# Delta rule by pairs of heads: two heads' chunk work side by side in shared tiles

## The chip, the cores and the metric

The kernel runs on one core of a Trainium2 chip. Times are device microseconds (us) of that core, from the start to the end of one execution. The core has a matrix engine (TensorE, PE in the profile, with its weight loads as PEld), a vector engine (VectorE, DVE), a scalar engine (ScalarE, ACT), GpSimd (POOL) and SyncE (SP), which here only issues DMAs. Each engine works through its own queue in order.

## The reference

One decoder layer over 1024 positions of width 1024, batch 1: half a SwiGLU step, a mixer, half a SwiGLU step, and a final RMSNorm. The change touches only the mixer's first half, eight heads of a gated delta rule with keys and values of width 128 (the other half, a state-space scan of 16 heads, and the SwiGLU steps stay as they are):

```python
qkv = jax.nn.silu(causal_dwconv(gdn_qkv, gdn_conv_w))
beta = jax.nn.sigmoid(gdn_b)
g = -jnp.exp(gdn_a_log) * jax.nn.softplus(gdn_a + gdn_dt_bias)
o = gated_delta_rule(q, k, v, g, beta)
o = rms_norm(o, gdn_norm_w) * jax.nn.silu(gdn_z)
...
# S_t = exp(g_t) (I - beta_t k_t k_t^T) S_{t-1} + beta_t k_t v_t^T,  o_t = S_t^T q_t
decay = jnp.exp(jnp.where(incl, gc[..., :, None] - gc[..., None, :], -jnp.inf))
a_low = jnp.where(strict, beta[..., :, None] * kk * decay, 0.0)
t_inv = triangular_solve(eye + a_low, eye)
...
def step(state, inp):
    v_new = u_c - w_c @ state
    o = qd_c @ state + qk_c @ v_new
    state = state * gt_c + kd_c.T @ v_new
```

Queries and keys are normalised first. The kernel works on chunks of 128 positions, eight per head, rather than the reference's 64; the recurrence over chunks is the same.

## The kernel before

The program is written as engine instructions on tiles. A planner puts the instructions of each engine in a fixed order: what comes earlier in the source goes first, and what is ready by its reckoning may fill the gaps. It also sets the semaphores, and a tile with fewer buffers than its uses makes a new use wait for the release of an old one.

The projections of the normalised input, which is kept in `hhi` and `hlo` (the value rounded, and the rest), are made by `proj_half`: a half is 128 output channels by 512 positions, eight steps of three matmuls (`mm3`, L121 to L123) into one bank `ps_pj`, of which there are three. Weights come by `next_w`, two tiles of 128 channels at a time, in the order of `w_seq`: for a head first Q and K, then V and the gate Z. `conv_silu` (L781 to L789) projects two halves, evicts each with two ScalarE operations (L781, L782), adds three taps on VectorE (L784, 128x1024 each) and applies SiLU.

For each head h in turn, the loop in the section `gdn` then does the following.

1. **Decays** (L1125 to L1130): the running log decay `g_scr[h]` is loaded into `dt`, spread over the partitions; `qe` is its exponential times `qt`; GpSimd masks `dt` (L895) and ScalarE takes the exponentials of its eight blocks (L1129).
2. **Keys' products** (L1141 to L1155): for two chunks at a time into one bank `ps_mx` (there are two) kk and kq; VectorE takes the trace (`jd`, L1145), forms `br` and makes `u`, the triangular matrix, and writes the masked kq products back into `dt`.
3. **Inverse**: the diagonal 32x32 blocks of `u` go through DRAM (`fs_u`, `fu`) into a layout in which a substitution of 31 steps, two VectorE operations each (L1205, L1207), solves all of them at once; the result returns through `fs_x` to `lv` and `u` (L1210, L1217, L1218). Then the blocks are joined, first to 64, then to 128, by four runs of small products (L1225/L1226, L1232 to L1234, L1246, L1251) with copies between them.
4. **Transposes**: of `qt` for its norm (L1173), of the values into `vr` (L1186, L1188), of the keys into `kd` (L1262, L1264).
5. **Scan** over the eight chunks (L1274 to L1296): the product of keys with the state `st`, the correction `rr`, the product with the inverse, `vn`, the output `po` (one bank `ps_oo`) and the new state `sn`; the output replaces the values in `vr`.
6. **Norm** (L1302 to L1307): sums of squares, a reciprocal root by Newton steps, and the store of `vr` to `mix_scr`.

All products of steps 2 to 5 are in full fp32, and each such product of 128 columns is two TensorE instructions. Tiles of pool `g2` (`qe`, `dt`, `u`, `vr` and the small ones) have two buffers, `kt` three, `qt` two (tag `xst`); `vt_`, `kd`, `fu`, `fx`, `lv` have one. So the scan of one head stands beside the projections and the inverse of the next.

After the last projections `out_start` begins the output projection: `group_tile` for the four groups of state-space heads, `pair_prep` and `pair_tile` for two halves of four delta rule heads. These read `mix_scr` and the gates `z_scr` through `out_load` (tiles `nat`, `zg` in a pool of their own, `natp`) and add to `xt2`, eight blocks of x from a pool `x2`.

Of the kernel before, what the change touches and what calls it, by code (L numbers as in the profile page):

```python
# [11 lines left out]
F32 = mybir.dt.float32  # L12
# [9 lines left out]
P = 128  # L22
# [18 lines left out]
NEG = -1.0e30  # L41


@with_exitstack
def kernel(
# [1007 lines left out]
    def out_load(grp):  # L1053
        nat = natp.tile([P, NB, 256], F32, name="nat")
        nc.sync.dma_start(out=nat, in_=mix_scr[grp])
        zg = natp.tile([P, 2, L], F32, name="zg")
        for j in range(2):
            nc.sync.dma_start(out=zg[:, j], in_=z_scr[2 * grp + j])
        return nat, zg
# [40 lines left out]
    natp = cn.enter_context(tc.tile_pool(name="natp", bufs=1, side="right", reuse_waits="tile"))  # L1100
    with ExitStack() as cg:
        g1 = cg.enter_context(tc.tile_pool(name="gdn1", bufs=1, reuse_waits="tile"))
        g2 = cg.enter_context(tc.tile_pool(name="gdn2", bufs=2, reuse_waits="tile"))
        for h in range(GH):
            hl = h % 2
            qt = gp.tile([P, L], F32, name="qt", tag="xst", bufs=2)
            kt = g2.tile([P, L], F32, name="kt", bufs=3)
            vt_ = g1.tile([P, L], F32, name="vt_")
            wa = next_w()
            conv_silu(g1, wa, 0, cw_g, h, qt)  # L1110
            conv_silu(g1, wa, 1, cw_g, 8 + h, kt)
            wa = next_w()
            conv_silu(g1, wa, 0, cw_g, 16 + h, vt_)
            zc = g1.tile([P, L], F32, name="zc")
            for half in range(2):
                A.activation(out=zc[:, half * 512:(half + 1) * 512], in_=proj_half(*wa, 1, half),
                             func=AF.Silu)
            nc.sync.dma_start(out=z_scr[h], in_=zc)
            if h == GH - 1:
                out_start()  # L1120


            qe = g2.tile([P, L], F32, name="qe")
            dt = g2.tile([P, NB, P], F32, name="dt")
            nc.sync.dma_start(out=dt, in_=g_scr[h].rearrange("(b t) -> b t", b=NB).partition_broadcast(P))  # L1125
            A.activation(out=qe, in_=dt.rearrange("p b t -> p (b t)"), func=AF.Exp)
            causal(dt, (NB,))
            for b in range(NB):
                A.activation(out=dt[:, b], in_=dt[:, b], func=AF.Exp, bias=ngc[:, b, h:h + 1])  # L1129
            V.tensor_tensor(out=qe, in0=qe, in1=qt, op=ALU.mult)  # L1130


            u = g2.tile([P, NB, P], F32, name="u")
            tk = g2.tile([P, NB], F32, name="tk")
            br2 = g2.tile([P, NB], F32, name="br2")
            for b0 in range(0, NB, 2):
                pg = psum("mx")
                b2 = slice(b0, b0 + 2)
                for i in range(2):
                    bs = slice((b0 + i) * P, (b0 + i + 1) * P)  # L1140
                    T.matmul(pg[:, i * 256:i * 256 + P], lhsT=kt[:, bs], rhs=kt[:, bs], start=True, stop=True)  # L1141
                    T.matmul(pg[:, i * 256 + P:(i + 1) * 256], lhsT=kt[:, bs], rhs=qt[:, bs],
                             start=True, stop=True)
                    jd = g1.tile([P, P], BF16, name="jd")
                    V.scalar_tensor_tensor(out=jd, in0=pg[:, i * 256:i * 256 + P], scalar=1.0, in1=ident,  # L1145
                                           op0=ALU.mult, op1=ALU.mult,
                                           accum_out=tk[:, b0 + i:b0 + i + 1])
                V.tensor_scalar(out=tk[:, b2], in0=tk[:, b2], scalar1=EPS, scalar2=None, op0=ALU.add)
                V.reciprocal(out=br2[:, b2], in_=tk[:, b2])
                V.tensor_tensor(out=br2[:, b2], in0=br2[:, b2], in1=beta[:, b2, h], op=ALU.mult)  # L1150
                for i in range(2):
                    V.scalar_tensor_tensor(out=u[:, b0 + i], in0=pg[:, i * 256:i * 256 + P],
                                           scalar=br2[:, b0 + i:b0 + i + 1], in1=dt[:, b0 + i],
                                           op0=ALU.mult, op1=ALU.mult)
                V.tensor_tensor(out=dt[:, b2],  # L1155
                                in0=pg.rearrange("p (i c) -> p i c", i=2)[:, :, P:2 * P],
                                in1=dt[:, b2], op=ALU.mult)
            fs_u = dram.tile([4, NB, 32, 32], F32, name="fs_u", bufs=2)
            for j in range(4):
                js = slice(32 * j, 32 * j + 32)  # L1160
                nc.sync.dma_start(out=fs_u[j].rearrange("b s l -> s b l"), in_=u[js, :, js])


            vr = g2.tile([P, NB, P], F32, name="vr")
            ssq = g2.tile([P, NB], F32, name="ssq")
            rin = g2.tile([P, NB], F32, name="rin")
            rsqrt_into(g2, rin, tk, "rst")
            V.tensor_tensor(out=rin, in0=rin, in1=tk, op=ALU.mult)
            for half in range(2):
                pt = psum("mx")  # L1170
                for i in range(4):
                    b = half * 4 + i
                    T.transpose(pt[:, i * P:(i + 1) * P], qt[:, b * P:(b + 1) * P], ident)  # L1173
                for i in range(4):
                    b = half * 4 + i
                    jk = g2.tile([P, P], BF16, name="jk", bufs=1)
                    A.activation(out=jk, in_=pt[:, i * P:(i + 1) * P], func=AF.Square,
                                 accum_out=ssq[:, b:b + 1])
            cq = g2.tile([P, NB], F32, name="cq")
            V.tensor_scalar(out=cq, in0=ssq, scalar1=EPS * P, scalar2=EPS * EPS * P,  # L1180
                            op0=ALU.mult, op1=ALU.add)
            for half in range(2):
                pt = psum("mx")
                for i in range(4):
                    b = half * 4 + i
                    T.transpose(pt[:, i * P:(i + 1) * P], vt_[:, b * P:(b + 1) * P], ident)  # L1186
                hb = slice(half * 4, half * 4 + 4)
                V.tensor_tensor(out=vr[:, hb], in0=pt.rearrange("p (i c) -> p i c", i=4),  # L1188
                                in1=rin[:, hb].unsqueeze(2).to_broadcast([P, 4, P]), op=ALU.mult)


            fs_x = dram.tile([4, NB, 32, 32], F32, name="fs_x", bufs=2)
            fu = g1.tile([P, 32, 32], F32, name="fu")
            for q in range(4):
                nc.sync.dma_start(out=fu[32 * q:32 * q + 32], in_=fs_u.rearrange("j b s l -> (j b) s l"))
            fx = g1.tile([P, 8, 32], F32, name="fx")
            ft = g1.tile([P, 80], F32, name="ft")
            fxf = fx.rearrange("p s l -> p (s l)")
            G.memset(fxf, 0.0)
# [286 lines left out]
```

## Time and profile before

| | us |
|---|---|
| median of 3 runs | 2312.65 |
| lowest, highest | 2310.45, 2313.74 |
| the profiled execution | 2311.71 |
| its span, first to last instruction | 2309.8 |
| VectorE in the substitution, lines 1205 and 1207, 248 operations each | 51.9 and 53.5 |
| scan: VectorE's `rr`, `vn`, `sn` (lines 1276, 1281, 1293) | 19.6, 22.3, 16.6 |
| projections of the mixer, lines 121 to 123 with `hhi` and `hlo`, 2496 matmuls | 332.8, 332.2, 334.3 |

A row of groups gives line, engine, operation, what is written and read, count, busy time, mean of one in ns, and the idle time of the engine ahead of it. A row of the timeline gives start, length, engine, line, operation and count; matmuls are pipelined, so their lengths overlap and the distance of their starts tells what one costs. In a stretch of the view by windows the columns are length, busy time and count of each engine, granted clock, DMA share and rate.

### The profile page before, as it was taken

The numbers are of one execution on the slowest core, as the hardware profiler recorded it, in microseconds if no ns is written. First come the engines' busy times: TensorE is split into PE (matmuls) and PEld (weight loads), VectorE is DVE, ScalarE is ACT, GpSimd is POOL, SyncE is SP. The second block draws the span as 40 slices with busy tenths as digits, with TensorE's granted clock in tenths as the row PEclk, the third lists the DMA queues.
The fourth block names the chain that finished last, engine by engine and source line by source line (L and its number), as shares of the span: only waits on it lengthen the run. The fifth ranks groups of instructions, "written<-read, shape, count | busy, mean of one in ns | idle before, by whom it ended". The sixth has DMA issues, their size and how long they took to land.

```text
span 2309.8 us, 31485 instructions
## 1 busy us (share of the span) xinstructions
PE 2275.9 (99%) x11766; PEld 1868.7 (81%) x11766; DVE 1726.7 (75%) x3349; ACT 1096.0 (47%) x1990; POOL 53.6 (2%) x125
## 2 busy tenths in 40 slices
PE   7999999999999999999999999999999999999998
PEld 5788888888878888888888888888878888888886
DVE  7977776767765675668778888778698777766787
ACT  7433333343367785864455556422543333334344
POOL 0000000000000100000000000000000000000000
PEclk9999999999999999999999999999999999999999
DMA  3333332573652322222333222335223333329456
GB/s 111 125 114 103 105 108 98 175 279 129 220 180 78 92 92 74 72 86 74 83 101 82 73 83 61 116 98 192 91 83 116 111 102 105 109 88 349 141 156 214
DMA packets 220957, 281.33 MB, mean 122 GB/s; under 512 B 47008, under 2 KB 153564, under 8 KB 219780
## 3 DMA queue, kind: packets, MB, share of 16 engines
q1 hardware_dynamic: 220548, 279.23, 37.4%
q8 instruction: 92, 1.51, 0.3%
q14 instruction: 61, 0.50, 0.1%
q0 software_dynamic: 256, 0.10, 0.0%
HBM read 211.55 MB, written 67.73 MB: 121 GB/s over the span
## 4 chain that ended last, share of the span: by engine, by line
PE 89%; DVE 5%; ACT 2%; DMA 1%; issue 1%; SPq 0%; POOL 0%; DVEq 0%; ACTq 0%
PE ps_pj L123 11%; PE ps_pj L122 10%; PE ps_pj L121 10%; PE ps_pj L332 6%; PE ps_pj L334 6%; PE ps_pj L333 6%; PE ps_mx L332 3%; PE ps_mx L334 3%; PE ps_mx L333 3%; PE ps_pj L553 2%; PE ps_pj L554 2%; PE ps_pj L552 2%; PE ps_oo L334 2%; PE ps_oo L333 2%; PE ps_oo L332 2%; PE ps_sc L552 1%
## 5 line engine op out<-in xcount | busy, mean ns | idle before, releaser
L123 PE MATMUL ps_pj<-hhi,wlo 128*128 128x512 f32 x832 | 334.3, 402 | 0.0
L121 PE MATMUL ps_pj<-hhi,whi 128*128 128x512 f32 x832 | 332.8, 400 | 0.4 <-ACT gsb L826 0.4
L122 PE MATMUL ps_pj<-hlo,whi 128*128 128x512 f32 x832 | 332.2, 399 | 0.0
L334 PE MATMUL ps_pj<-bh,al 128*128 128x512 f32 x688 | 267.9, 389 | 0.0
L333 PE MATMUL ps_pj<-bl,ah 128*128 128x512 f32 x688 | 267.8, 389 | 0.0
L332 PE MATMUL ps_pj<-bh,ah 128*128 128x512 f32 x688 | 267.5, 390 | 0.0
L121 PEld LDWEIGHTS ps_pj<-hhi,whi 128*128 128x128 f32 x832 | 156.7, 188 | 28.8 <-ACT gsb L826 0.8
L123 PEld LDWEIGHTS ps_pj<-hhi,wlo 128*128 128x128 f32 x832 | 156.7, 188 | 28.5 <-issue 0.7
L122 PEld LDWEIGHTS ps_pj<-hlo,whi 128*128 128x128 f32 x832 | 156.7, 188 | 27.9
L239 ACT CAST ah<-wst 128x512 fp32r<-128x512 f32 x88 | 54.6, 622 | 210.8 <-PE ps_oo L333 125.3
L239 ACT CAST hid<-hraw 128x1024 fp32r<-128x1024 f32 (+1 forms) x84 | 82.3, 981 | 145.5 <-PE ps_oo L554 60.6
L333 PEld LDWEIGHTS ps_pj<-bl,ah 128*128 128x128 f32 x688 | 129.2, 188 | 26.8
L334 PEld LDWEIGHTS ps_pj<-bh,al 128*128 128x128 f32 x688 | 129.1, 188 | 26.6
L332 PEld LDWEIGHTS ps_pj<-bh,ah 128*128 128x128 f32 x688 | 128.9, 188 | 26.6
L315 DVE TENSOR_TENSOR as<-wst 128x512 f32<-128x512 f32 x220 | 145.0, 684 | 2.1 <-DMA wst<-in_ffn_w_up_dram 1.8
L240 DVE TENSOR_TENSOR al<-as,ah 128x512 fp32r<-128x512 f32 x220 | 141.0, 685 | 5.0 <-ACT ah L239 4.5
L332 PE MATMUL ps_mx<-bh,ah 128*128 128x512 f32 x352 | 138.6, 396 | 3.8 <-ACT m L341 1.4
L333 PE MATMUL ps_mx<-bl,ah 128*128 128x512 f32 x352 | 138.2, 393 | 0.4 <-DVE bl L240 0.4
L334 PE MATMUL ps_mx<-bh,al 128*128 128x512 f32 x352 | 137.7, 391 | 0.3 <-DVE al L240 0.3
L239 ACT CAST ah<-as 128x512 fp32r<-128x512 f32 x220 | 125.0, 617 | 20.8 <-DVE as L315 20.8
L240 DVE TENSOR_TENSOR hid<-hraw,hid 128x1024 fp32r<-128x1024 f32 (+1 forms) x84 | 95.0, 1131 | 32.8 <-ACT hid L239 32.5
L341 ACT COPY m<-ps_pj 128x512 f32<-128x512 f32 x88 | 51.5, 588 | 123.1 <-PE ps_pj L334 120.9
(448 smaller groups left out, 5118.9 us busy)
## 6 DMA issues: line engine op xcount, KB each, us to landing
hraw<-hid_scr SPq DMA_DIRECT2D x70, 512.0 KB, 4.4
hid_scr<-hs SPq DMA_DIRECT2D x110, 256.0 KB, 2.3
wst<-in_ffn_w_down_dram SPq DMA_DIRECT2D x50, 512.0 KB, 4.7
wst<-in_ffn_w_gate_dram SPq DMA_DIRECT2D x22, 1024.0 KB, 5.7
wst<-in_ffn_w_up_dram SPq DMA_DIRECT2D x22, 1024.0 KB, 5.4
wst<-in_w_in_dram SPq DMA_DIRECT2D x36, 512.0 KB, 5.2
hid_scr<-sg SPq DMA_DIRECT2D x44, 256.0 KB, 2.0
keep<-in_ffn_w_down_dram SPq DMA_DIRECT2D x20, 512.0 KB, 6.2
```

Source lines behind the costliest of these rows:

```text
L121: T.matmul(o, lhsT=wh, rhs=mh, start=first, stop=False)
L122: T.matmul(o, lhsT=wh, rhs=ml, start=False, stop=False)
L123: T.matmul(o, lhsT=wl, rhs=mh, start=False, stop=last)
L239: return (A.copy(out=hi, in_=src), V.tensor_tensor(out=lo, in0=src, in1=hi.bitcast(F32), op=ALU.subtract))
L240: V.tensor_tensor(out=lo, in0=src, in1=hi.bitcast(F32), op=ALU.subtract))
L315: V.tensor_tensor(out=t, in0=v[0], in1=v[1], op=v[2])
L332: T.matmul(bank, lhsT=wh[:, k], rhs=bh[:, k], start=a, stop=False, skip_group_check=True)
L333: T.matmul(bank, lhsT=wh[:, k], rhs=bl[:, k], start=False, stop=False, skip_group_check=True)
L334: T.matmul(bank, lhsT=wl[:, k], rhs=bh[:, k], start=False, stop=z, skip_group_check=True)
L341: A.copy(out=t, in_=bank)
L552: T.matmul(bank, lhsT=hh, rhs=wh, start=first and k == 0, stop=False, skip_group_check=True)
L553: T.matmul(bank, lhsT=hh, rhs=wl, start=False, stop=False, skip_group_check=True)
```

## The change

The loop over eight heads becomes a loop over four pairs. All tiles of a head's steps 1 to 6 get a dimension for the two heads, and the order of a pair is: Q and K of the first head, Q and K of the second, V of both from one weight tile, and then gates. The gates are taken from earlier pairs by `Z_BEHIND`: none in the first pair, those of heads 0 and 1 in the second, 2 and 3 in the third, 4 to 7 in the last.

- Keys' products: both banks `ps_mx` are filled, one for each head, sixteen instructions in a row; the small operations on `tk` and `br2` work on both heads.
- Substitution: the same 62 operations on twice the columns. The DMAs through DRAM stay of the same size each, twice as many for a pair.
- Levels of the inverse: runs of 16 chunks in place of 8; the two last levels fill two banks `ps_sc`.
- Scan: the products of both heads stand next to each other in one bank, and `vn` is one operation; `rr` and `sn` are two. `behind` adds a wait: the first product of a run waits for the results of both heads.
- Buffers: `qe`, `dt`, `u`, `vr`, `vt_` lie in a new pool `g3` with one buffer each, for two heads; `kt` alternates between `g3` and `g1`.
- `natp` and `x2` are gone. `nat` and `zg` take over the tiles of `vt` and `kt` in `g3`, the x blocks those of `qe`, `dt`, `u` and `vr`, loaded by `load_x2` at the same place of the program.

The core of the diff:

```diff
+Z_BEHIND = ((), (0,), (2,), (4, 6))
...
-    for h in range(GH):
-        w_seq.append((COL_Q + h * P, COL_K + h * P))
-        w_seq.append((COL_V + h * P, COL_GZ + h * P))
+    for h in range(0, GH, 2):
+        w_seq.extend((COL_Q + i * P, COL_K + i * P) for i in (h, h + 1))
+        w_seq.append((COL_V + h * P, None))
+        w_seq.extend((COL_GZ + i * P, None) for i in Z_BEHIND[h // 2])
...
-        nat = natp.tile([P, NB, 256], F32, name="nat")
+        nat = g3.tile([P, NB, 256], F32, name="nat", tag="vt")
...
-    natp = cn.enter_context(tc.tile_pool(name="natp", bufs=1, side="right", reuse_waits="tile"))
+    g3 = cn.enter_context(tc.tile_pool(name="gdn3", bufs=1, side="right", reuse_waits="tile"))
...
-        for h in range(GH):
+        for pr in range(GH // 2):
+            h0 = 2 * pr
+            kt2 = (g1, g3)[pr % 2 == 0].tile([P, 2, L], F32, name="kt", tag="kt")
+            kts = [kt2[:, i] for i in range(2)]
+            for i, h in enumerate((h0, h0 + 1)):
+                wa = next_w()
+                qts.append(gp.tile([P, L], F32, name="qt", tag="xst", bufs=2))
+                conv_silu(g1, wa, 0, cw_g, h, qts[-1])
+                conv_silu(g1, wa, 1, cw_g, 8 + h, kts[i])
             wa = next_w()
+            vt2 = g3.tile([P, 2, L], F32, name="vt_", tag="vt")
+            for i in range(2):
+                conv_silu(g1, wa, i, cw_g, 16 + h0 + i, vts[i])
+            for hz in Z_BEHIND[pr]:
+                wa = next_w()
+                for i in range(2):
+                    zc = g1.tile([P, L], F32, name="zc")
...
-            qe = g2.tile([P, L], F32, name="qe")
-            dt = g2.tile([P, NB, P], F32, name="dt")
+            qe = g3.tile([P, 2, L], F32, name="qe")
+            dt = g3.tile([P, 2, NB, P], F32, name="dt")
...
+                pgs = [psum("mx") for _ in range(2)]
...
-                t = ft[:, 0:r * n].rearrange("p (s l) -> p s l", l=n)
-                V.tensor_tensor(out=t, in0=fx[:, 0:r, j:j + 1].to_broadcast([P, r, n]),
-                                in1=fu[:, j:j + 1, j + 1:32].to_broadcast([P, r, n]), op=ALU.mult)
+                t = ft[:, 0:2 * r * n].rearrange("p (i s l) -> p i s l", i=2, l=n)
+                V.tensor_tensor(out=t, in0=fx[:, :, 0:r, j:j + 1].to_broadcast([P, 2, r, n]),
+                                in1=fu[:, :, j:j + 1, j + 1:32].to_broadcast([P, 2, r, n]), op=ALU.mult)
...
+            def behind(m, made):
+                tc.add_manual_dep(m.ins, made.ins.name, mybir.DependencyInfo(
+                    mybir.DependencyClass.Sync, mybir.DependencyReason.DATA), reason="one run of products")
...
                 if st is not None:
                     p1 = psum("sc")
-                    T.matmul(p1[:, 0:P], lhsT=kt[:, bs], rhs=st, start=True, stop=True)
+                    for i in range(2):
+                        m = T.matmul(side(p1, i), lhsT=kts[i][:, bs], rhs=st[:, i], start=True, stop=True)
+                        if i == 0:
+                            behind(m, st_made)
+                    po = psum("oo")
+                    for i in range(2):
+                        T.matmul(side(po, i), lhsT=qe[:, i, bs], rhs=st[:, i], start=i == 0, stop=False,
+                                 skip_group_check=True)
...
-                V.tensor_scalar(out=vn, in0=p2[:, 0:P], scalar1=br2[:, b:b + 1], scalar2=None, op0=ALU.mult)
+                V.tensor_tensor(out=vn, in0=both(p2), in1=br2[:, :, b:b + 1].to_broadcast([P, 2, P]), op=ALU.mult)
...
-    xp2 = c2.enter_context(tc.tile_pool(name="x2", bufs=1, side="right", reuse_waits="tile"))
-    xt2 = blocks(xp2, "xt2")
+    def load_x2():
+        for i, tag in enumerate(("qe", "dt", "u", "vr")):
+            t = g3.tile([P, 2, D], F32, name="xt2", tag=tag)
+            for j in range(2):
+                xt2[2 * i + j] = t[:, j]
+                nc.sync.dma_start(out=t[:, j], in_=x_scr[:, 2 * i + j])
```

More of the change, by code (lines that the diff above doesn't have):

```diff
@@ L1192 @@
[L1192 to L1198, printed above, removed]
+                for i in range(2):
+                    V.tensor_tensor(out=vr[:, i, hb], in0=pts[i].rearrange("p (c l) -> p c l", c=4),
+                                    in1=rin[:, i, hb].unsqueeze(2).to_broadcast([P, 4, P]), op=ALU.mult)
@@ L1289 @@
-                    sn = g2.tile([P, P], F32, name="sn")
+                    for i in range(2):
+                        T.matmul(side(p3, i), lhsT=kd[:, i, b], rhs=vn[:, i], start=True, stop=True)
+                if st is None:
+                    po = psum("oo")
+                for i in range(2):
+                    T.matmul(side(po, i), lhsT=dt[:, i, b], rhs=vn[:, i], start=st is None and i == 0,
+                             stop=i == 1, skip_group_check=True)
+                if b < NB - 1:
+                    sn = g2.tile([P, 2, P], F32, name="sn")
@@ L1383 @@
     wb = out_w(0, 1)
-    for b in range(NB):
-        nc.sync.dma_start(out=xt2[b], in_=x_scr[:, b])
+    load_x2()
     for b in range(NB):
```

302 lines of the change are left out of this document (162 added, 140 removed).

## The prediction

> **What bounds the kernel now.** I read the page first: the span, the busy times, the clock, the chain.
>
> ```profile
> span 2309.8 us, 31485 instructions
> PE 2275.9 (99%) x11766; PEld 1868.7 (81%) x11766; DVE 1726.7 (75%) x3349; ACT 1096.0 (47%) x1990; POOL 53.6 (2%) x125
> PEclk9999999999999999999999999999999999999999
> PE 89%; DVE 5%; ACT 2%; DMA 1%; issue 1%; SPq 0%; POOL 0%; DVEq 0%; ACTq 0%
> ```
>
> TensorE is occupied for 99% of the span at the full granted clock and holds 89% of the chain that ended last. The view by stretches shows how this stands in the part that changes. The columns are length, then the busy time of PE, PEld, DVE, ACT and POOL, the clock, the DMA share and GB/s. The first row is heads 4 and 5, from the keys' products of head 4 to those of head 6; the second is the last head's tail with the output projection beginning.
>
> ```profile
> 1246.00:1374.50 128.50, 128.28 (x871) 104.70 (x870) 102.23 (x342) 67.18 (x159) 5.62 (x18) 1.00 0.28 74
> 1440.00:1562.00 122.00, 121.00 (x821) 98.26 (x820) 95.98 (x254) 43.30 (x108) 0.30 (x1) 1.00 0.34 106
> ```
>
> Two heads take 128.5 us and TensorE is free for 0.2 us of them. So nothing done on VectorE is worth anything by itself: what counts is the time that a TensorE instruction holds its place in the queue. For that I read the timeline of TensorE, by starts (ends overlap, since matmuls are pipelined).
>
> ```profile
> 1084.31 0.40 PE L122 MATMUL ps_pj<-hlo,whi 128*128 128x512 f32 x1
> 1084.54 0.39 PE L1274 MATMUL ps_sc<-sn,kt 128*128 128x128 f32 x2
> 1084.77 0.39 PE L1284 MATMUL ps_oo<-sn,qe 128*128 128x128 f32 x2
> 1084.91 0.48 PE L123 MATMUL ps_pj<-hhi,wlo 128*128 128x512 f32 x1
> 1085.22 0.40 PE L121 MATMUL ps_pj<-hhi,whi 128*128 128x512 f32 x1
> 1085.46 0.41 PE L1279 MATMUL ps_sc<-rr,u 128*128 128x128 f32 x2
> 1085.62 0.48 PE L122 MATMUL ps_pj<-hlo,whi 128*128 128x512 f32 x1
> 1085.94 0.40 PE L123 MATMUL ps_pj<-hhi,wlo 128*128 128x512 f32 x1
> ...
> 1256.30 0.48 PE L122 MATMUL ps_pj<-hlo,whi 128*128 128x512 f32 x1
> 1256.71 1.14 PE L1246 MATMUL ps_sc<-lv,u 64*64 64x64 f32 x16
> 1257.79 0.50 PE L123 MATMUL ps_pj<-hhi,wlo 128*128 128x512 f32 x1
> 1258.12 0.39 PE L121 MATMUL ps_pj<-hhi,whi 128*128 128x512 f32 x1
> ```
>
> A projection matmul of 512 columns takes 0.23 us from start to start (1084.31 to 1084.54). Half a scan product (each is two instructions) takes 0.115 (1084.54 to 1084.77 for two). Four of them between projections cost 1085.22 - 1084.31 - 2 x 0.23 = 0.45 us, almost only their own 4 x 0.11. Two cost 1085.94 - 1085.22 - 2 x 0.23 = 0.26 for 0.22. So a scan run pays 0.01 to 0.04 us for being a run. The 16 products of the inverse's last level cost 1258.12 - 1256.30 - 2 x 0.23 = 1.36 us, where one takes 1.14 - 0.22 over 16, 0.058 us, together 0.92: that run pays 0.44 us.
>
> **The change part by part.** *TensorE.* The numbers of projections, products and transposes stay; only the number of runs halves. Scan: a head has 23 runs (7 + 8 + 8), 184 in all, 92 fewer; at 0.03 us, 2.8 us. Keys' products: 64 groups of four become 16 of sixteen; 48 fewer, 1.4 us. Inverse: four levels' runs per head, 32, become 16; at 0.44 us, 7 us. The sum is 11 us. The bounds: nothing if the fixed part of a run grows with the run, and 22 us, the fixed parts of all runs of before, if they went altogether. I take 11, by the rows.
>
> [...]
>
> *VectorE* gets cheaper, hidden under TensorE, but it sets the length of the chain of a pair, and that is what can spoil the change. The operations:
>
> ```profile
> L1205 DVE TENSOR_TENSOR ft<-fx,fu 128x60 f32<-128x60 f32 (+24 forms) x248 | 51.9, 209 | 5.4
> L1281 DVE TENSOR_SCALAR vn<-ps_sc,br 128x128 f32<-128x128 f32 x64 | 22.3, 348 | 10.7 <-PE ps_sc L1279 10.1
> L1155 DVE TENSOR_TENSOR dt<-ps_mx,dt 128x256 f32<-128x256 f32 x32 | 13.4, 419 | 0.2
> L784 DVE SCALAR_TENSOR_TENSOR kt<-pre,cols,kt 128x1024 f32<-128x1024 f32 x24 | 30.7, 1279 | 0.0
> ```
>
> From 128 to 256 columns an operation grows from 0.35 to 0.42 us, so 0.55 ns per column. A step of the substitution has 50 columns on average by the loop's sizes, which double: +0.03 us at that rate, +0.05 at the nearly 1 ns per column that the convolution's 1024 columns show (1.28 us, less the fixed part). With 0.05 for each of the 62 steps a pair's substitution is 3 us longer than a head's.
>
> *The new waits.* The tiles `dt`, `qe`, `u`, `vr` had two buffers each, one head apiece. Now one buffer holds both heads of a pair, so the decays of pair p+1 are loaded only when the scan of pair p is over, its keys' products write `u` and `dt` only then, and `qt` (two buffers, both used by a pair) comes free for the next projection only after them. Before, head h+2 waited for head h, and the chain of one head ran beside the next one's. I follow head 4 through the queues of SyncE, ScalarE and VectorE.
>
> ```profile
> 1224.29 0.35 SPq L1125 DMA_DIRECT2D dt<-g_scr  x1
> ...
> 1264.23 1.81 SPq L1161 DMA_DIRECT2D fs_u<-u  x4
> 1267.50 1.71 SPq L1195 DMA_DIRECT2D fu<-fs_u  x4
> ...
> 1304.81 2.53 SPq L1210 DMA_DIRECT2D fs_x<-fx  x4
> ...
> 1351.30 0.34 SPq L1125 DMA_DIRECT2D dt<-g_scr  x1
> ```
>
> ```profile
> 1237.23 2.15 ACT L1129 ACTIVATE dt<-dt,ngc 128x128 f32<-128x128 f32 x7
> ```
>
> ```profile
> 1246.77 0.29 DVE L1145 SCALAR_TENSOR_TENSOR jd<-ps_mx,ident 128x128 bf16<-128x128 f32 x1 [4.16 <-PE ps_mx L1142]
> ...
> 1277.86 0.18 DVE L1205 TENSOR_TENSOR ft<-fx,fu 128x31 f32<-128x31 f32 x1
> ...
> 1315.32 0.44 DVE L1219 STREAM_TRANSPOSE lv<-lv 128x256 f32<-128x256 f32 x1
> ...
> 1325.65 0.34 DVE L1281 TENSOR_SCALAR vn<-ps_sc,br 128x128 f32<-128x128 f32 x1
> ...
> 1333.00 0.35 DVE L1281 TENSOR_SCALAR vn<-ps_sc,br 128x128 f32<-128x128 f32 x1 [0.58 <-PE ps_sc L1279]
> 1334.15 0.35 DVE L1293 SCALAR_TENSOR_TENSOR sn<-sn,egt,ps_sc 128x128 f32<-128x128 f32 x1 [0.81 <-PE ps_sc L1288]
> ```
>
> Keys 17.5 us (1246.8 to 1264.2), trip through DRAM 13.6, substitution 27, second trip 10.5, levels 10.3, scan 25.7 (to 1351.30, where the end of the scan frees `dt` for the next load): 104.5 us. For a pair: keys stay at 18, since VectorE's part doubles but the other head's levels, which ran in between, are gone. The first trip has 8 + 8 DMAs issued in place of 4 + 4, at 0.45 us each: +3.5. The substitution gets +3 and loses some 5 of the other head's scan between its steps: -2. The second trip has 8 and 16 issues in place of 4 and 8, at 0.63 and 0.45 us, partly overlapped: +5. The levels have double runs and double copies, +5, less 1.5 for the other head's keys: +3.5. In the scan a block has two `rr`, two `sn` and a wide `vn`: +0.27 + 0.27 + 0.07 and two more half products, 0.22, makes 0.83 us x 8 = 6.5, less about 3.5 of other work: +3. This gives 104.5 + 13 = 117.5. Ahead of it stand the load of `dt`, exponentials and mask: 15.1 us for one head (1224.29 to 1239.38). A pair has twice the exponentials (2.5 us more), but its first products and traces need no `dt`, and the first `u` needs only the first blocks; I take 10, between 8 and 17. **One cycle of a pair: 127.5 us.**
>
> What TensorE has to do meanwhile: the same 128.5 us less 2.8, so 125.7. It can run ahead by three banks of `ps_pj`, 3 x 24 x 0.23 = 16 us, and by the products themselves, some 9 (64 half products and 16 transposes at 0.11), against 22 us from the first key product until `qt` is free (the 18 above and 4 for its transposes): 3 us in all. With two cycles before the last projections, the stall is 2 x 127.5 - 2 x 125.7 - 3, under 1 us, and about 2 us for each further us of the cycle. That is a narrow balance.
>
> *Behind the added waits.* `behind` makes the first product of a run wait for both heads' results, 0.27 us later than the first head's; queued behind it stand projections. It costs nothing while projections are issued ahead of it, up to 56 x 0.27 = 15 us where there are none. *End.* After the last gates TensorE has the output products:
>
> ```profile
> L121 PE MATMUL ps_pj<-whi,mtt 128*128 128x512 f32 x192 | 77.5, 404 | 0.8 <-DVE xa L1343 0.8
> ...
> L1285 PE MATMUL ps_oo<-vn,dt x128: 270/275/377, 1075.8 to 1561.1; 128*128 128x128 f32 x128
> ...
> 1568.85 0.56 SPq L1307 DMA_DIRECT2D mix_scr<-vr  x1
> ...
> mix_scr<-vr SPq DMA_DIRECT2D x8, 512.0 KB, 3.7
> ...
> nat<-mix_scr SPq DMA_DIRECT2D x4, 1024.0 KB, 4.9
> ```
>
> Three such groups are 576 x 0.23 = 132 us, and the pair's own products 37 (125.7 less 384 x 0.23 of projections). Against them stand a chain of 117, by an estimate 18 more among the output's own VectorE work (of the 122 us of the second stretch VectorE is busy for 96), and 26 to bring heads 6 and 7 back: 7.5 from the scan's last product at 1561.1 (the end of the first and last start in its row) to the store, 3.7 and 4.9 for the two DMAs, 10 for transposes and gates. 169 against 161: covered, by little. The x blocks take over the tiles of `qe`, `dt`, `u`, `vr`, so they too load only after the last scan; these 8 loads stand behind the same wait as before (the region of the old pools). ScalarE has half of each stretch free, so its wider copies cost nothing.
>
> Sum: -11 + 1 = -10 us on the profiled execution's 2311.71 (span 2309.8 and 1.9 around it); the median of the runs is 0.9 us above that. **2303 us.** A measurement can tell 0.2%, 4.6 us, from no change.
>
> **The rivals.** *The single buffers set the pace (slower).* If the contention that I subtracted (5 + 1.5 + 3.5 us) is replaced by the next pair's convolutions, three operations of 1.28 us for each, the cycle is 135 to 140 and TensorE stands still for 15 to 25 us at the start of the projections of pairs 2 and 3: 2317 to 2327. It decides from a cycle of 132.5 us on, where the stall eats the 11. For it speaks that VectorE is 80% busy in these stretches; against it that its work falls. [...]
>
> *Nothing to see.* Runs get dearer as they get longer, or a stall of some 6 to 14 us returns the gain: 2308 to 2317. *The end becomes the bound:* the last pair's chain of 135 us is 10 longer than assumed and the output tiles of heads 4 to 7 wait: +3 to +10 on any of these. *More than 11:* the fixed parts vanish altogether, 22 us: 2291.
>
> **How the numbers follow.** Covered, faster: 0.48, 2296 to 2308. Nothing to see: 0.21. Pace set by the single buffers, or the end, slower: 0.31, up to 2330. The range is 2294 to 2329: from halfway into the larger gain to all but the worst of the stalls.
>
> **What would show it.** Right: TensorE's free time in the stretch of two pairs stays under 1 us, runs of eight scan instructions between projections, 32 at the levels. Wrong: rows of the first projection `ps_pj<-hhi` waiting for a convolution's tile, and gaps ahead of the keys' products that end with the scan of the pair before; VectorE idle meanwhile; or a second load of `dt` more than 128 us after the first.

## The result and the profile after

The changed kernel takes **2366.26 us** (median of 5 runs, 2362.89 to 2370.76) against 2310.78 us for the kernel before, measured beside it. The ratio is 1.0239, with a 95% interval of 1.0228 to 1.0250: slower by 55 us, where 2303 us and a range of 2294 to 2329 had been forecast. The profiled execution is the fastest of the five, 2362.89 us, so the traces below account for 51 us, not for 55.

The page of the changed kernel, the same lines as shown of before:

```profile
span 2361.1 us, 31003 instructions
PE 2292.0 (97%) x11766; PEld 1883.5 (80%) x11766; DVE 1678.7 (71%) x2909; ACT 1069.2 (45%) x1928; POOL 51.5 (2%) x101
PEclk9999999999999999999989899999999999999999
PE 85%; DVE 8%; ACT 4%; DMA 1%; issue 1%; POOL 0%; SPq 0%; DVEq 0%; ACTq 0%
```

VectorE has 440 operations fewer and 48 us less to do, as intended. But TensorE is no longer always occupied (97%), two slices show a lower clock, and VectorE holds 8% of the chain that ended last in place of 5%. The view by stretches of the changed kernel shows where (length, busy time of PE, PEld, DVE, ACT, POOL, then clock, DMA share and GB/s):

```profile
1150.00:1200.00 50.00, 37.47 (x200) 30.73 (x199) 30.32 (x101) 19.86 (x71) 3.04 (x2) 0.84 0.26 67
1300.00:1350.00 50.00, 37.50 (x188) 31.21 (x187) 30.05 (x99) 20.77 (x71) 3.12 (x2) 0.80 0.26 69
...
1600.00:1650.00 50.00, 44.66 (x265) 36.67 (x265) 34.37 (x75) 14.01 (x47) 0.00 (x0) 0.93 0.38 127
1650.00:1700.00 50.00, 46.35 (x211) 37.26 (x210) 32.16 (x55) 18.93 (x31) 0.00 (x0) 0.97 0.34 126
```

Twice TensorE stands still for 12.5 us and runs at a reduced clock besides. These are the keys' products of pairs 1 and 2. VectorE is idle there too (30 of 50 us busy), so neither is at its limit: they wait for each other. The other two rows are the last pair's scan and what follows it. TensorE's waits in the changed kernel, over the whole span (in all, times, longest):

```profile
PE ps_mx L1157 <- DVE dt L1175: 17.5, 8, 3.0
PE ps_pj L123 <- DVE xt L1432: 8.5, 2, 5.3
...
PE ps_mx L1199 <- DVE dt L1175: 5.7, 3, 2.7
```

One such place in TensorE's timeline, by starts:

```profile
1171.75 0.39 PE L125 MATMUL ps_pj<-hhi,wlo 128*128 128x512 f32 x1
1175.11 0.49 PE L1157 MATMUL ps_mx<-kt 128*128 128x128 f32 x2 [2.97 <-DVE dt L1175]
...
1179.90 0.46 PE L1157 MATMUL ps_mx<-kt 128*128 128x128 f32 x2 [2.66 <-DVE dt L1175]
...
1191.32 1.94 PE L1199 MATMUL ps_mx<-ident,qt 128*128 128x128 f32 x8 [2.66 <-DVE dt L1175]
...
1195.95 0.80 PE L123 MATMUL ps_pj<-hhi,whi 128*128 128x512 f32 x1 [0.78 <-ACT qt L785]
1196.55 0.63 PE L124 MATMUL ps_pj<-hlo,whi 128*128 128x512 f32 x1
```

The last projection that fits starts at 1171.75. Then the three banks `ps_pj` are full with the next pair's first projections, which may not leave them before `qt` is free (the wait of L123 for ScalarE's `qt` at 1195.95). The keys' products come in steps that fill both banks `ps_mx`, so each step waits for VectorE to end the one before. Where the projections go on, the next 512-column matmul follows after 0.60 us instead of 0.23; the clock granted from 1195 to 1200 is 0.50.

Why so late? The loads of `dt` in SyncE's queue give the cycle of a pair, which the prediction had put at 127.5 us:

```profile
1164.03 1.54 SPq L1138 DMA_DIRECT2D dt<-g_scr  x2
...
1190.61 3.78 SPq L1182 DMA_DIRECT2D fs_u<-u  x8
...
1244.15 5.22 SPq L1241 DMA_DIRECT2D fs_x<-fx  x8
...
1309.77 0.80 SPq L1138 DMA_DIRECT2D dt<-g_scr  x2
```

It is 145.7 us. VectorE's rows of the same pair split it: the first `u`, the first operation of the substitution, the transpose that opens the levels, the first `vn` of the scan.

```profile
1173.92 0.60 DVE L1172 SCALAR_TENSOR_TENSOR u<-ps_mx,br,dt 128x128 f32<-128x128 f32 x2
...
1212.17 1.28 DVE L787 SCALAR_TENSOR_TENSOR kt<-pre,cols,kt 128x1024 f32<-128x1024 f32 x1
1213.37 0.21 DVE L1235 TENSOR_TENSOR ft<-fx,fu 128x62 f32<-128x62 f32 x1
...
1260.00 0.71 DVE L1251 STREAM_TRANSPOSE lv<-lv 128x512 f32<-128x512 f32 x1 [3.29 <-DMA lv<-fs_x]
...
1278.80 0.42 DVE L1336 TENSOR_TENSOR vn<-ps_sc,br 128x256 f32<-128x256 f32 x1
```

| us | predicted | measured |
|---|---|---|
| load of `dt` to first `u` | 10 | 9.9 |
| keys (to the store of `fs_u`) | 18 | 16.7 |
| first trip (to the substitution) | 17.1 | 22.8 |
| substitution | 25 | 30.8 |
| second trip | 15.5 | 15.9 |
| levels | 13.8 | 18.8 |
| scan (to the next load) | 28.7 | 31.0 |
| cycle | 127.5 | 145.7 |

The predicted terms of this table add up to 128.1: the prediction's changes to the 104.5 us of a head are 13.5 and not the 13 that it added, and its rounded stages hold another 0.1.

The bill up to the end of the projections is the last row of that kind in each trace, before and changed:

```profile
1438.52 0.40 PE L123 MATMUL ps_pj<-hhi,wlo 128*128 128x512 f32 x1
...
1660.37 0.39 PE L123 MATMUL ps_pj<-whd,mt 128*128 128x512 f32 x1
```

```profile
1468.38 0.40 PE L125 MATMUL ps_pj<-hhi,wlo 128*128 128x512 f32 x1
...
1711.36 0.39 PE L125 MATMUL ps_pj<-whd,mt 128*128 128x512 f32 x1
```

30 us are lost before the last projection (the first row of each fence), 21 more before the last output product with `mt` (the second row). Behind that the two traces run alike.

### The profile page after: what moved, and what is told of

Its sections match the earlier page's. It is cut to its first block, busy times and chain, and to the rows that moved or that the text cites. A ratio compares the mean times of both kernels' runs of the same rounds, so it can differ in the third digit from the quotient of the medians.

```text
span 2361.1 us, 31003 instructions
## 1 busy us (share of the span) xinstructions
PE 2292.0 (97%) x11766; PEld 1883.5 (80%) x11766; DVE 1678.7 (71%) x2909; ACT 1069.2 (45%) x1928; POOL 51.5 (2%) x101
## 4 chain that ended last, share of the span: by engine, by line
PE 85%; DVE 8%; ACT 4%; DMA 1%; issue 1%; POOL 0%; SPq 0%; DVEq 0%; ACTq 0%
PE ps_pj L123 9%; PE ps_pj L125 9%; PE ps_pj L124 9%; PE ps_pj L334 6%; PE ps_pj L336 6%; PE ps_pj L335 6%; PE ps_mx L334 3%; PE ps_mx L336 3%; PE ps_mx L335 3%; PE ps_pj L555 2%; PE ps_pj L556 2%; PE ps_pj L554 2%; PE ps_oo L335 2%; PE ps_oo L334 2%; PE ps_oo L336 2%
## 5 line engine op out<-in xcount | busy, mean ns | idle before, releaser
L123 PE MATMUL ps_pj<-hhi,whi 128*128 128x512 f32 x832 | 332.3, 399 | 2.7 <-ACT qt L785 2.3
L123 PEld LDWEIGHTS ps_pj<-hhi,whi 128*128 128x128 f32 x832 | 157.3, 189 | 33.8 <-ACT qt L785 3.4
```

Of the source, the lines that this page charges most:

```text
L123: T.matmul(o, lhsT=wh, rhs=mh, start=first, stop=False)
```

## The experiments

The theory, **single buffers**: one buffer of `dt`, `u` and the queries for two heads ties each pair to the end of the scan before; the cycle of 146 us stands against 126 of TensorE work. Rivals: the waits of `behind`; the gates' order; the halved clock; the keys' products in both banks.

### Without the added waits

```diff
-                        if i == 0:
-                            behind(m, st_made)
...
-                    if st is not None and i == 0:
-                        behind(m, rr_made)
```

> The change without its added waits: the two calls of `behind` are left out, nothing else. Theory 'single buffers' (a pair's chain from the load of dt to the end of its scan takes 146 us where TensorE has about 126 us of work, so TensorE runs dry before the keys' products of pairs 1 and 2): the waits are a side matter, 2362 to 2369 us, gaps of TensorE in the stretches 1150 to 1200 and 1300 to 1350 of about 12.5 us each as in the changed kernel. Rival 'added waits' (56 waits of 0.27 us or more, each with projections queued behind it): 2350 or less, since 15 us go.

Measured: **2353.3 us**, 1.0184 of before (1.0167 to 1.0201), 13 us less. Both expectations missed, the rival by less. The first and last start of the masked products of one pair's scan (count; shortest, median and longest duration in ns; first and last start) tell how, in the changed kernel and then without the waits:

```profile
L1344 PE MATMUL ps_oo<-vn,dt x32: 274/275/362, 1279.8 to 1309.4; 128*128 128x128 f32 x32
```

```profile
L1340 PE MATMUL ps_oo<-vn,dt x32: 275/275/361, 1277.3 to 1304.1; 128*128 128x128 f32 x32
```

29.6 us against 26.8. TensorE is never idle in this scan (31.00 us busy from 1279 to 1310); with the waits, its products simply come later among the projections. Nothing is lost on TensorE, but the scan is 3 us longer, and here the scan is part of the cycle, which is 142.6 us without the waits. Of the 12 us between the two traces, 6 stand before the last projection (it starts at 1462.3) and 6 behind it. The gaps stayed: 38.86 and 38.65 us busy in the two stretches that had 37.47 and 37.50.

### The gates of the pair's own heads

```diff
-Z_BEHIND = ((), (0,), (2,), (4, 6))
+Z_BEHIND = ((0,), (2,), (4,), (6,))
```

> The change with the gates of each pair's own heads, one weight tile per pair, in place of none, one, one, two. Theory 'single buffers': TensorE's work per cycle of pairs 1 and 2 stays as it is, so the gaps stay at about 12.5 us; the first pair's chain starts up to 22 us later and the last pair has 22 us less beside it: 2366 to 2390. Rival 'gates' order' (the gaps come from cover that stands in the wrong place): the gaps shrink by more than half, 2330 to 2350.

Measured: **2371.9 us**, 1.0264 (1.0248 to 1.0279). The stretches of this kernel (length, PE busy, clock, DMA):

```profile
1150.00:1200.00 50.00, 46.63 (x293) 1.00 0.24 75
1200.00:1250.00 50.00, 43.29 (x195) 0.90 0.20 48
1300.00:1350.00 50.00, 42.49 (x254) 0.89 0.22 74
1350.00:1400.00 50.00, 44.99 (x197) 0.83 0.18 48
```

The four rows lack 22.6 us of TensorE time, the changed kernel's two rows 25.0. The gap is spread, not removed: cover in another place doesn't shorten the cycle, which is 146.7 us here and then 152.8. The order of the gates was not the fault.

### Products that keep the clock up in the gaps

```diff
+                if pr > 0 and b0 > 0:
+                    po = psum("oo")
+                    for _ in range(10):
+                        T.matmul(po[:, 0:P], lhsT=kts[1][:, b0 * P:b0 * P + P],
+                                 rhs=kts[1][:, b0 * P:b0 * P + P], start=True, stop=True)
```

> The change with 10 more products (20 instructions, about 2.3 us) into the bank ps_oo after each of the later three steps of the keys' products of pairs 1 to 3; their results are not used. They fill the waits of 2.7 us between the steps, so that TensorE's clock stays up. Theory 'single buffers, chain bound by VectorE': the steps are VectorE's, the time stays within 2358 to 2374 though the clock is 1.0. Rival 'cold clock' (the gaps of some 2.7 us halve the clock, and the halved clock makes the chain and the projections behind it longer): the granted clock of the two stretches rises from 0.80 to 0.84 to above 0.95 and 10 to 18 us go, 2348 to 2356.

Measured: **2364.8 us**, 1.0233 (1.0217 to 1.0248), against 2366.3 without. The clock of both stretches rose to 0.93, not above 0.95, from 0.84 and 0.80, and the cycle fell only to 143.4 us. So in these gaps the halved clock is in the main a symptom. What a full clock would be worth isn't shown: it was not reached, and the added products take TensorE's time too.

### Keys' products head by head

```diff
-                pgs = [psum("mx") for _ in range(2)]
-                for i in range(2):
-                    for c in range(2):
+                for i in range(2):
+                    pg = psum("mx")
+                    for c in range(2):
```

> The change with the keys' products made head by head: a step of two chunks of one head takes one bank ps_mx, so that the next step's products are made while VectorE works on the last; the small operations on tk and br2 are by head again. Buffers, scan and `behind` stay. Theory 'single buffers': TensorE's waits between the steps (8 us for each of pairs 1 and 2) shrink, VectorE has 12 more small operations per pair, and a pair's cycle falls from 146 us by some 5: 2350 to 2360 us, the gaps stay for the most part. Rival 'the keys' products take both banks' (the whole gap is the ping-pong between the two engines): the gaps of 12.5 us fall below 4 and the clock stays above 0.95: 2335 or less.

Measured: **2355.9 us**, 1.0191 (1.0175 to 1.0208): 10 us less than the changed kernel. The number is the one that the theory had, the place is not. TensorE is busy for 41.56 and 42.24 us of the two stretches, so a third of each gap went, but at a clock of 0.83 and 0.73; the cycle is 144.1 and then 146.3 us, not 5 us shorter, and the last projection starts at 1465.9, only 2.5 us earlier. The larger part of what was gained stands behind it, and why is not shown. The two banks in one step are at most a small part of the stall.

### Two buffers for dt, u and the queries

```diff
-            qe = g3.tile([P, 2, L], F32, name="qe")
-            dt = g3.tile([P, 2, NB, P], F32, name="dt")
+            dt = g3.tile([P, 2, NB, P], F32, name="dt", bufs=2)
...
-            u = g3.tile([P, 2, NB, P], F32, name="u")
+            u = g3.tile([P, 2, NB, P], F32, name="u", bufs=2)
...
+                qts.append(gp.tile([P, L], F32, name="qt", tag="xst", bufs=2) if pr % 2 == 0 else
+                           g1.tile([P, L], F32, name="qt", tag="qt", bufs=2))
...
+                V.tensor_tensor(out=qts[i], in0=e, in1=qts[i], op=ALU.mult)
```

> The change with two buffers for each of dt, u and the queries of a pair: the queries are multiplied by the decays in place (no qe), the exponentials pass through the tile vr, the values are transposed during the second trip through DRAM, kd takes over the tile of fu, zc that of pre, fx that of lv. The order of the pair's products and `behind` stay. Theory 'single buffers': the keys' products of a pair stand beside the scan of the one before, the two gaps of 12.5 us and their low clock go, the last projection ends at 1440 to 1450 us instead of 1469, and the time is 2300 to 2325. Rivals 'the keys' products take both banks' and 'the chain is too long among its neighbours': the gaps stay in large part, 2345 or more.

Measured: **2322.9 us**, 1.0056 (1.0040 to 1.0072): 43 of the 55 us are back, and 36 us of that stand before the last projection, which starts at 1432.5 in place of 1468.4. The same two stretches, and the scans of pairs 0 and 1, in this kernel:

```profile
1150.00:1200.00 50.00, 49.77 (x287) 41.60 (x287) 37.78 (x115) 26.09 (x78) 2.23 (x4) 1.00 0.41 111
1300.00:1350.00 50.00, 47.84 (x220) 38.67 (x219) 40.33 (x76) 29.80 (x66) 2.77 (x6) 1.00 0.38 107
```

```profile
L1347 PE MATMUL ps_oo<-vn,dt x32: 275/275/275, 1139.4 to 1169.8; 128*128 128x128 f32 x32
L1347 PE MATMUL ps_oo<-vn,dt x32: 275/275/275, 1264.8 to 1296.4; 128*128 128x128 f32 x32
```

From the end of one scan to the end of the next it is 126.6 us: TensorE's work sets the pace again, and the clock is full. The scan itself is as long as in the changed kernel (30 us); it only stands beside the next pair's keys. The edit does more than add buffers: to make room it drops `qe`, moves the transposes of the values behind the second trip and loads the decays once more. So the 43 us belong to the whole of it; of the buffers, only that of `u` was tried alone.

### One buffer for u again

```diff
-            u = g3.tile([P, 2, NB, P], F32, name="u", bufs=2)
+            u = g3.tile([P, 2, NB, P], F32, name="u")
```

> `decoupled` with one buffer for u again (dt and the queries keep two): the keys' products, traces and exponentials of a pair may be made beside the scan of the one before, but its u is written only when the last products with the old u are done, about 1 us ahead of the scan's end. Theory 'single buffers': what is saved of the 146 us cycle is what stands ahead of the first u, 10 us, so a cycle of about 136 us stands against 126 of TensorE work, the gaps come back at some 10 us for pairs 1, 2 and in part 3, and the time is 2340 to 2352. Rival 'dt alone was the matter' (u's wait is hidden): the time of `decoupled`, 2321 to 2327.

Measured: **2341.2 us**, 1.0131 (1.0117 to 1.0146). The number is the one expected, the place is not. Scans of pairs 0 to 3, and two stretches, of this kernel:

```profile
L1347 PE MATMUL ps_oo<-vn,dt x32: 275/275/356, 1142.5 to 1171.3; 128*128 128x128 f32 x32
L1347 PE MATMUL ps_oo<-vn,dt x32: 275/275/366, 1285.5 to 1314.0; 128*128 128x128 f32 x32
L1347 PE MATMUL ps_oo<-vn,dt x32: 275/275/355, 1424.4 to 1456.8; 128*128 128x128 f32 x32
L1347 PE MATMUL ps_oo<-vn,dt x32: 275/275/356, 1583.9 to 1613.2; 128*128 128x128 f32 x32
```

```profile
1450.00:1500.00 50.00, 45.08 (x243) 36.50 (x242) 36.29 (x111) 22.46 (x64) 0.00 (x0) 0.97 0.54 173
1600.00:1650.00 50.00, 42.36 (x216) 33.86 (x214) 39.54 (x71) 16.49 (x38) 0.00 (x0) 0.97 0.49 169
```

The cycle is back at 142.7 and 142.8 us, more than the 136 expected. But with four query tiles the projections run ahead, and TensorE finds work: its last projection starts at 1430.0, no later than with two buffers of `u` (1432.5). So a long cycle alone does not stop TensorE; in the changed kernel it does, and there a projection waits for a free `qt` (1195.95). The debt is paid at the end, where the last pair's scan finishes at 1613 in place of 1597 and the output waits for it. One buffer of `u` costs 18 us; which of `dt`, the queries and the moved work brings the rest was not separated.

### Two buffers, without the added waits

> The kernel with two buffers (`decoupled`), and the calls of `behind` left out. If the added waits cost 13 us whatever the buffers are (as they did beside single buffers: 2366 to 2353), 2308 to 2312, no slower than the kernel before; if they only cost where a chain sets the pace (the cycle of a pair, the end), 2314 to 2319, since beside two buffers only the last pair's scan is such a place.

The edits of the first and the fifth experiment together. Measured: **2315.4 us**, 1.0019 (1.0010 to 1.0028). `behind` costs 7.5 us here, not 13. The number fits the second case, its reason does not: the last projection starts at 1426.7 in place of 1432.5, so most of the difference stands ahead of the last pair's scan. From scan to scan this kernel needs 125.6 us:

```profile
L1343 PE MATMUL ps_oo<-vn,dt x32: 275/275/377, 1139.8 to 1166.7; 128*128 128x128 f32 x32
L1343 PE MATMUL ps_oo<-vn,dt x32: 275/275/377, 1265.4 to 1292.3; 128*128 128x128 f32 x32
```

That is the 125.7 us of TensorE work that the prediction had for a pair.

### Added products in the last pair's inverse

The kernel with two buffers and no added waits has a dip of the clock of its own, beside the last pair's levels: half speed, while TensorE is recorded as busy (length, PE busy, clock, DMA).

```profile
1535.00:1540.00 5.00, 3.73 (x163) 0.74 0.78 299
1540.00:1545.00 5.00, 5.00 (x32) 0.50 0.10 15
1545.00:1550.00 5.00, 5.00 (x39) 0.50 0.49 197
1550.00:1555.00 5.00, 5.00 (x25) 0.56 0.29 94
```

What is missing in the first row are two short waits of the levels' products for VectorE's copies:

```profile
1536.87 0.24 PE L1268 MATMUL ps_sc<-lv 32*32 32x32 f32 x2 [0.79 <-DVE lv L1264]
1537.60 0.26 PE L1269 MATMUL ps_sc<-lv 32*32 32x32 f32 x1 [0.48 <-DVE lv L1264]
```

```diff
+            if pr == 3:
+                po = psum("oo")
+                with tc.issue_after(lm.ins):
+                    for _ in range(2):
+                        T.matmul(po, lhsT=ident, rhs=kts[0][:, 0:512], start=True, stop=True)
```

> `dec_nb` with five products of 128x512 in full fp32 (about 0.9 us each, results unused) in the last pair's inverse: one behind the products of the first level, two behind those of the second, two behind those of the third. In the kernels without them the granted clock falls to 0.50 at this place for some 17 us, though TensorE is shown as busy. Theory 'runs of small tiles count as idle': the clock of the stretch rises to above 0.85, 8 us of half clock are worth up to 7 us, and the 4.5 us of added products stand in part in waits: 2 to 5 us less than `dec_nb`. Rival 'the clock does not matter there, VectorE's chain sets the end': 0 to 4 us more than `dec_nb`.

Measured: **2310.8 us**, 0.9996 of before (0.9987 to 1.0005), 4.5 us less than without the added work, within the 2 to 5 of the first case. Two of the same stretches in this kernel:

```profile
1535.00:1540.00 5.00, 4.72 (x166) 1.00 0.91 334
1540.00:1545.00 5.00, 5.00 (x41) 1.00 0.06 22
```

With one product behind each level:

> `dec_nb_warm` with one added product behind each of the three levels in place of one, two and two: 1.8 us less of added work. If three products (2.7 us) keep the clock up, 2308 to 2310, below the kernel before by about 0.1%; if the clock falls to 0.50 again, 2314 to 2316 as `dec_nb` has it.

Measured: **2312.2 us**, 1.0002 (0.9993 to 1.0011). The clock stays at 1.00, but the time lies between the two cases. Less added work brought nothing more.

The same five products in the changed kernel itself:

> The changed kernel itself with the five added products of `dec_nb_warm` in the last pair's inverse, nothing else changed. If the halved clock at the runs of small tiles is a part of the change's own loss, independent of the buffers: 2 to 5 us less than the changed kernel's 2366, 2360 to 2364, and the clock of the stretch 1590 to 1660 rises from 0.95 to 1.00. If it only counts where TensorE has been made the bound again: 2365 to 2371.

Measured: **2368.5 us**, 1.0247 (1.0232 to 1.0261): no gain. The changed kernel's clock is 1.00 at these levels (1585 to 1615) with and without them. Its low clock after 1600 (0.77 and 0.55 in the two stretches of 5 us from 1635 to 1645) lies behind the last scan, at the wait of 5.3 us for the output's x tiles (L1432). So the halved clock at the levels is no part of the change's own loss. It stands in the kernels with two buffers of `u` (in the first of them 0.72 from 1540 to 1550 and 0.50 from 1550 to 1560), and with single buffers in `no_behind` (0.50 from 1574 to 1590, behind waits of 0.78 and 0.48 us at the same products); not in `one_u`, where the clock is 1.00 from 1550 to 1600 and TensorE is busy throughout.

### Real work in place of added products, twice

```diff
+            def values(half, after):
+                with tc.issue_after(after.ins):
+                    pts = [turned(vts[i], "mx", half) for i in range(2)]
```

> `dec_nb` with the transposes of the values held behind the products of the inverse's first and second level, eight behind each, in every pair: real work of the kernel at the place of the added products of `dec_nb_warm`. Theory 'runs of small tiles count as idle': the clock at the last pair's inverse stays above 0.85 and the time is 3 to 7 us below `dec_nb`, since no work is added. Rival: the transposes' evictions lengthen the chain of the pair (four operations of some 0.6 us on VectorE between the levels), 1 to 4 us more than `dec_nb`.

Measured: **2393.0 us**, 1.0351 (1.0338 to 1.0365), off both expectations by 74 us or more. A wait of TensorE in pair 0 of this kernel, and the stretch:

```profile
PE ps_sc L1262 <- DVE lv L1255: 16.9, 1, 16.9
```

```profile
1100.00:1150.00 50.00, 36.81 (x353) 0.66 0.10 16
```

Holding the transposes back made the planner put the first level 105 projections (24 us) earlier in TensorE's order in each of the first three pairs, and 18 output products earlier in the last. There it stands ahead of its own operands, the second trip through DRAM, and everything queued behind it waits, four times and 48.9 us in all.

```diff
+            if last_pair:
+                kd = g3.tile([P, 2, NB, P], F32, name="kd", tag="dt", bufs=2)
...
+                with tc.issue_after(lm.ins):
+                    kin = keys_in(0, "mx")
```

> `dec_nb` with real work at the same place: in the last pair the 16 transposes of the keys are held behind the products of the second and third level, eight each, and their tile is another buffer (that of dt from the pair before). No work is added. The static order puts the first level of this pair 18 output products (4 us) earlier among TensorE's instructions than in `dec_nb`. If the transposes keep the clock up and the earlier place costs a wait of up to 4 us: 2307 to 2312; if the clock falls all the same, 2315 to 2320.

Measured: **2323.5 us**, 1.0052 (1.0038 to 1.0067), worse than both cases. The first level, 18 output products earlier, left TensorE 1.98 us busy out of 5 (1530 to 1535), and behind that the clock was 0.53 for 5 us and 0.50 for 15 more.

## Why the prediction was wrong, point by point

**What bounds the kernel.** Right: TensorE was the bound, and VectorE's saving, 48 us by the page, bought nothing by itself.

**Half as many runs, -11.** The sign holds, the size only in part. Free of the single buffers a pair needs 125.6 us from scan to scan, as forecast. But the gain does not reach the end: with two buffers, no added waits and a full clock the time is that of before, with five added products in it, 4.5 us by the estimate of 0.9 us for each (two instructions of 0.115 us for every 128 columns). By an estimate from that, some 5 of the 11 us were there. The inverse's levels gave part of their 7. In the changed kernel the first level is one run of 64 instructions for 1264.96 - 1263.17 - 2 x 0.23 = 1.33 us, where two runs of 32 cost 0.83 each before (1253.84 - 1252.55 - 2 x 0.23). But the third level still stands as two runs of 16 (1269.07 and 1271.52), with projections between its two banks. Read in the same way, the four levels save some 0.3, 0.8, 0 and 0.2 us for a pair: 5 us in all, by an estimate from such rows. No run shows that the forecast's 0.44 us is paid once for each run, whatever its length, and what it consists of was not separated.

**The substitution's operations.** Right: a product of the substitution (L1235) on both heads takes 0.26 us by its group (32.4 us for 124) against 0.21, the 0.05 forecast. The stage was nevertheless 30.8 us long, not 25.

**The cycle of a pair, 127.5 us: this step failed.** The order of the waits was right, and the load of `dt`, the keys and the second trip came out within 1.5 us. Wrong were the first trip (+5.7), the substitution (+5.8), the levels (+5.0) and the scan (+2.3). From before's head the prediction had subtracted 10 us for the other head's work that would be gone. What moved into the first trip and the substitution was the next pair's convolutions and weight splits, 1.2 to 1.3 us each, in VectorE's fixed order: the row of L787 at 1212.17 is the last of five in a row ahead of the substitution, and ten more stand within it, 12.7 us, where head 4 of before had six. The rival had named the convolutions and stopped at 135 to 140. In the levels it is another thing: VectorE is busy there for some 7 of 18.8 us. The first product starts at 1263.49, 2.8 us after the transposed blocks were there, because TensorE has projections ahead of it (before, 0.4 us: 1315.76 to 1316.14). The scan's share was `behind`, priced at nothing because projections are issued ahead of it. That is true of TensorE, but it makes the scan 3 us longer, and a scan that is part of the cycle is paid in full. Two of the signs that the prediction had named for its being wrong are there: a second load of `dt` more than 128 us after the first, and a projection that waits for `qt`.

**Two us per us of cycle.** Right: 2 x 145.7 - 2 x 125.7 - 3 gives 37 us of stall, less what the runs gain. The trace lost 30 by the last projection.

**The end, covered by 8 us.** Wrong: its bound was the rival "the end becomes the bound", and by more than its 3 to 10. The last pair's load of `dt` stands at 1456.6 in the trace and its scan ends at 1631.7: 175 us, where the prediction had 117.5, 10 and 18, together 145. Both terms of this step were too small. The pairs before had taken 145.7 us where 127.5 were forecast, and the last one took 29 us more than they did, where the prediction had 18 for the output's own VectorE work. Its substitution alone lasts 47.6 us, against 30.8 in pair 1:

```profile
1517.27 0.21 DVE L1235 TENSOR_TENSOR ft<-fx,fu 128x62 f32<-128x62 f32 x1
...
1564.91 5.18 SPq L1241 DMA_DIRECT2D fs_x<-fx  x8
```

Its own operations are 15.8 us of that. Among them stand 33 additions to the output (L1411, 24.6 us) and four weight splits (4.9 us). All versions of the pairs have this late last scan, at 1581 to 1658 against 1561 before, and with `u` single most of the loss was there.

**The granted clock.** It fell to half in the stalls (0.50 from 1190 to 1200), where the longest waits were 2.7 to 3.0 us, with products between them. Yet with the clock in part kept up in the gaps (`warm`, 0.93) the time fell by no more than 1.5 us, and the cycle by 2.3: the chain more than the clock held TensorE back.

**The range** ended at 2329, since its upper end was about the single-buffer rival at a cycle of 140. The chance of 0.31 for slower had the right mechanism and too small a price.

## What to carry to other kernels

Merging two pipelined streams into one wide step halves the instructions (the substitution's 496 operations became 248), but a buffer that is now shared turns the overlap of two chains into their sum (here a cycle of 145.7 us, against 126.6 with two buffers): add up the whole chain from the release of the buffer to its next release, with what actually stands in the in-order queues then, and compare it with the bound engine's work for the same stretch. Contention seen in the old schedule must not be subtracted before naming what takes its place. A wait that costs its own engine nothing still lengthens the chain that it stands on (a scan of 29.6 us in place of 26.8); and where run-ahead hides a late chain, look for the debt at the end.

## What was not expected of the hardware

In the kernel with two buffers and no added waits, TensorE's clock fell to 0.50 at runs of 32x32 products with waits of only 0.5 and 0.8 us between them, 1.3 us idle out of 5, and stayed there for about 14 us (1540 to 1555) in which TensorE was recorded as busy 5.00 of 5.00. In the stalls of the changed kernel, where it fell too, the longest waits were 2.7 to 3.0 us. Five added products of 128x512, 4.5 us by the estimate above, kept the clock at 1.00 (1535 to 1560), and three did too. Small tiles alone did not bring the clock down: in the changed kernel the same runs stand among 512-column matmuls, TensorE is busy 5.00 of 5.00, and the clock is 1.00 (1585 to 1600). Whether the short waits or the lack of larger products among the small ones brought it down was not separated: both changed together.
